# Encoder block on one core: first score map's buffers over other memory, distance copies later in a tile, meta columns by a two-input operation, four output rows in flight

## The chip, the cores and the metric

The kernel runs on one core of one Trainium2 chip. The metric is device time in microseconds (us) of one execution; lower is better. The engines are called as the profile calls them: PE (TensorE, matmuls and transposes), DVE (VectorE), ACT (ScalarE), POOL (GpSimd), and SP (SyncE), whose queue issues most DMAs.

## What is computed

One encoder block on 1024 tokens of width 1024, float32, with 16 meta tokens put in front. Two attention branches share one input: branch A is differential attention over all 1040 keys (4 heads, two score maps each), branch B is windowed attention with sinks (8 heads). Each branch is gated, both are added, and a SwiGLU network follows.

```python
h = concatenate([meta, x])                         # 1040 x 1024
p = rms_norm(h, norm_mix) @ w_in                   # qa ka va | qb kb vb | gate a, gate b
# branch A, head by head (two maps, m = 0 and m = 1)
s_m = q_m @ k_m.T * scale - slope * dist           # dist = |i - j|, 0 for meta keys
attn = softmax(s_0) - lam * softmax(s_1)
y_a = rms_norm(attn @ v, subln_g) * (1 - lambda_init)
# branch B: keys within 128 tokens and the meta keys, sink in the softmax
y_b = windowed_gqa(qb, kb, vb, sink)
h = h + (sigmoid(ga) * (y_a @ w_ba) + sigmoid(gb) * (y_b @ w_bb)) @ w_o
f = rms_norm(h, norm_ffn)
h = h + (silu(f @ w_ff_gate) * (f @ w_ff_up)) @ w_ff_down
out = rms_norm(h, norm_final)[16:]                 # 1024 rows of 1024
```

## The kernel before

Every float32 product is made of three matmuls of a high and a low part (fp32r); ACT makes the high part, DVE or POOL the low one. The large products follow Strassen's scheme with seven products instead of eight. The stages, by the time of the profile: projections and branch B up to about 275 us; branch A's attention together with the gate projections, 266 to 609 us; the branch products and the output projection to about 778 us; gate and up products of the feed-forward network to 1207 us; the down product, with the final norm and the output, to the end.

**Branch A** goes over 4 heads times 8 tiles of 128 queries. `scores_a(h, t)` makes the two maps of a tile, m = 1 first: PE writes three chunks of scores (352, 352 and 336 keys, L1049), two of them into the one pair of PSUM banks `two`, the third into one of three banks `sc`. DVE adds the distance bias and takes the minimum (L1052 for the two chunks, L1056 for the third), ACT takes the exponential (L1060). After m = 0, DVE combines both maps into the buffer of m = 0 (L1066) and copies the last 16 columns, the meta keys, twice behind it (L1070). A tile later `transpose_a` turns the result on PE (L1081); ACT and DVE split it (L1084, L1085), and PE multiplies it with the values (L1094).

The buffers of m = 1 come in turn from the pool `apool`. Those of m = 0 are two fixed tiles, `s0s` (`as0_0`, `as0_1`). `apool` lies where the pool of branch B (`bpool`) lay before it; where a new tile covers an old one, its first writer waits for the last user of the old tile. The order of allocation in `apool` thus decides what a tile waits for. In the kernel before, `s0s` comes behind the room of the transposed maps (`at`).

L1056 needs the distances of the last 336 keys in a form of their own, `far_m`, three tiles in turn. POOL fills them from `dist` (`far_copy`, L999), for a tile two tiles ahead; a copy waits until DVE has read the tile's content before.

**The gate projections** run in between: PE's order is written out by hand (`SLOTS`, one letter for a step: s scores, g a quarter of a gate product, t transposes, n values), with 63 gate products of 12 matmuls (L937). POOL makes their operands `wopg` (`weights_g`: sums at L816 and L817, a cast at L835, a low part at L836), from weights that SP loads (L795). The list `made_g` holds the low parts in order. Outside the orders written by hand a scheduler places the instructions, by a simulated timeline; `tc.issue_after(x)` puts what follows behind x.

**The end**: the down product's last step (p = 4) is finished row tile by row tile in `finish_last`: a sum of squares on ACT (L1843), the factor on POOL (L1870, L1871), then the two halves of an output row `o` on DVE (L1874) and ACT (L1876), each stored by its own DMA. Four earlier row tiles are finished in `evict`. Both take `o` from two buffers.

Of the kernel before, what the change touches and what calls it, by code (L numbers as in the profile page):

```python
# [9 lines left out]
F32 = mybir.dt.float32  # L10
# [4 lines left out]
ALU = mybir.AluOpType  # L15
# [4 lines left out]
P = 128  # L20
S = 1024
D = 1024
NM = 16
L = S + NM
DC = D // P
L_ROW = 1088
NT = S // P
# [13 lines left out]
SLOTS = "ssgsggntssgsggntgnt", "ssggsggntssgsggntgnt", "ssgsgnssgtsgntgnt"  # L41
N_PRE = 6
ON_ACT = (1, 6), (1, 7)
LAST_B = ("T1", 4), (5, "V0"), (5, "T2"), ("T2", 6), (7, "V1"), (7, "V2")
SLOTS_LAST = "ggggntgntnt"
S_BUFS = (2, 2)
# [31 lines left out]
def encoder_block(ctx: ExitStack, tc: tile.TileContext, x, meta, norm_mix, w_in, lq1, lk1, lq2, lk2,  # L78
                  subln, sink, w_ba, w_bb, w_o, norm_ffn, w_g, w_u, w_d, norm_final, out, dbg=None):
    nc = tc.nc  # L80
# [675 lines left out]
    apool, close_apool = pool("apool")  # L756
# [41 lines left out]
    sums_g, keys_a, raws_g, values_in, turned_t, made_g = {}, [], [], [], {}, []  # L798
# [190 lines left out]

    far_m = [(gstage if i > 1 else apool).tile([P, 336], F32, name=f"far_m{i}") for i in range(3)]  # L990
    apool.tile([P, 32], F32, name="apool_pad")
    apool.tile([P, 9, 2, 256], F32R, tag="at", name="at_room", bufs=AT_BUFS)

    def far_copy(n):
        if n < AH * NT:
            with ExitStack() as after:
                if n == 3:
                    after.enter_context(tc.issue_after(made_g[min(5, len(made_g) - 1)].ins))
                nc.gpsimd.tensor_copy(far_m[n % 3][:, 0:S - 704], dist[:, 1600 - n % NT * P:1600 - n % NT * P + S - 704])  # L999

    for i in range(3):
        nc.gpsimd.memset(far_m[i][:, S - 704:], 0.0)
        if i < 2:
            far_copy(i)
    s0s = [apool.tile([P, 9 * P], F32, name=f"as0_{i}") for i in range(2)]
    def load_a(h):
        p = kvpool
        qs, ks = [None, None], [None, None]
# [22 lines left out]
    def scores_a(h, t, ld, s):  # L1031
        slope = 2.0 ** -(2 * (h + 1))
        qs, ks, _ = ld
        nm = f"{h}_{t}"
        mn = small.tile([P, 2, 4], F32, tag="amn", name=f"amn_{nm}")
        dn = small.tile([P, 2], F32, tag="adn", name=f"adn_{nm}")
        if t % 4 == 0:
            sum_a[h, t // 4] = small.tile([P, 4], F32, tag="asum", name=f"asum_{nm}")
        first_sum = sum_a[h, t // 4][:, t % 4:t % 4 + 1]
        u0 = 896 - t * P  # L1040
        far = far_m[(h * NT + t) % 3]
        far_copy(h * NT + t + 2)
        for m in (1, 0):
            s[m] = s0s[t % 2] if m == 0 else apool.tile([P, L], F32, tag="s1", name=f"as1_{nm}", bufs=S_BUFS[1])
            two = psum2.tile([P, 2, 512], F32, tag="two", name=f"aps2_{nm}_{m}", bufs=1)
            for i, (k0, n) in enumerate(A_CHUNKS):
                ps = two[:, i] if i < 2 else bank(psum2, "sc", f"aps_{nm}_{m}", SC)
                for vv in range(2):
                    nc.tensor.matmul(ps[:, :n], qs[m][:, t * P:(t + 1) * P], ks[m][:, vv, k0:k0 + n],  # L1049
                                     start=(vv == 0), stop=(vv == 1))  # L1050
                if i == 1:
                    nc.vector.tensor_tensor_reduce(s[m][:, 0:2 * n].rearrange("p (a k) -> p a k", a=2), two[:, :, :n],  # L1052
                                                   dist[:, u0:u0 + 2 * n].rearrange("p (a k) -> p a k", a=2), slope, far_a,
                                                   ALU.add, ALU.min, mn[:, m, 0:1])
                elif i == 2:
                    nc.vector.tensor_tensor_reduce(s[m][:, k0:k0 + n], ps[:, :n], far, slope, mn[:, m, 0:1],  # L1056
                                                   ALU.add, ALU.min, mn[:, m, 1:2])
                if i < 2:
                    yield
            nc.scalar.activation(s[m][:, 0:L], s[m][:, 0:L], AF.Exp, bias=mn[:, m, 1:2], scale=-1.0,  # L1060
                                 accum_out=dn[:, 1:2] if m else first_sum)
            if m:
                nc.vector.reciprocal(dn[:, 1:2], dn[:, 1:2])
            yield
        nc.vector.tensor_scalar(dn[:, 0:1], first_sum, dn[:, 1:2], neglam, ALU.mult, ALU.mult)
        nc.vector.scalar_tensor_tensor(s[0][:, 0:L], s[1][:, 0:L], dn[:, 0:1], s[0][:, 0:L], ALU.mult, ALU.add)  # L1066
        with ExitStack() as after:
            if (h, t) == (0, 0):
                after.enter_context(tc.issue_after(made_g[min(5, len(made_g) - 1)].ins))
            nc.vector.tensor_copy(s[0][:, L:L + 2 * NM].rearrange("p (a k) -> p a k", a=2),  # L1070
                                  s[0][:, S:L].unsqueeze(1).broadcast_to([P, 2, NM]))

    def transpose_a(h, t, s, at_):
        i = t % 2
# [85 lines left out]
    for n in range(AH * NT + T_LAG):  # L1160
# [3 lines left out]
        if n < AH * NT:  # L1164
            h, t = divmod(n, NT)
# [289 lines left out]
    nf = len(order_f)  # L1455
# [375 lines left out]
    def evict(p, u):  # L1831

        half, col = TARGET[p]
        t, cols = 4 * half + u, slice(col * 512, col * 512 + 512)
        if p != 4 or not u:
            nc.vector.tensor_tensor(y[:, t, cols], y[:, t, cols], sets[BANKS[p]][u], ALU.add)
        yield
        if p in (2, 3, 7, 4):
            if t not in sums:
                sums[t] = upool.tile([P, 2], F32, name=f"ss_o{t}")  # L1840
            sq = upool.tile([P, 512], F32, tag="sq", name=f"sq_{t}_{col}", bufs=2)
            src = sets[BANKS[p]][u] if p == 4 and u else y[:, t, cols]
            nc.scalar.activation(sq, src, AF.Square, accum_out=sums[t][:, col:col + 1])  # L1843
            if p == 4:
                yield from finish_last(t, src)
                return
            yield
        if p == 7:

            nc.vector.tensor_tensor(y[:, t, cols], y[:, t, cols], nfin[:, cols], ALU.mult)  # L1850
            nc.vector.tensor_scalar(sums[t][:, 1:2], sums[t][:, 1:2], D * EPS, None, ALU.add)
        if p != 3:
            return
        ss = sums[t]
        o = upool.tile([P, D], F32, tag="o", name=f"o_{t}", bufs=2)
        r = small.tile([P, 1], F32, tag="rstd", name=f"rstd_o{t}")
        nc.vector.tensor_tensor(r, ss[:, 0:1], ss[:, 1:2], ALU.add)
        nc.vector.tensor_scalar(r, r, 1.0 / D, EPS, ALU.mult, ALU.add)
        nc.gpsimd.tensor_tensor(r, r, neg_half[:, 0:1], ALU.pow)
        yield  # L1860
        for i in range(2):
            at = slice(i * 512, i * 512 + 512)
            nc.vector.scalar_tensor_tensor(o[:, at], y[:, t, at], r, nfin[:, at], ALU.mult, ALU.mult)
        yield
        nc.sync.dma_start(out[t * P:(t + 1) * P, :], o)

    def finish_last(t, src):
# [2 lines left out]
        nc.gpsimd.tensor_scalar(r, ss[:, 0:1], ss[:, 1:2], 1.0 / D, ALU.add, ALU.mult)  # L1870
        nc.gpsimd.tensor_tensor(r, r, neg_half[:, 0:1], ALU.pow)  # L1871
        yield
        o = upool.tile([P, D], F32, tag="o", name=f"o_{t}", bufs=2)
        nc.vector.scalar_tensor_tensor(o[:, 0:512], src, r, nfin[:, 0:512], ALU.mult, ALU.mult)  # L1874
        nc.sync.dma_start(out[t * P:(t + 1) * P, 0:512], o[:, 0:512])
        nc.scalar.activation(o[:, 512:], y[:, t, 512:], AF.Copy, scale=r)  # L1876
# [7 lines left out]
    pending, running = [], []  # L1884
    for n in range(nf, len(steps)):
        p, j = steps[n][1]
        if n < nf + 4:

            prepare()
        while late:  # L1890
# [69 lines left out]
```

## Time and profile before

| | |
|---|---|
| median of 3 runs | 1417.67 us (1417.59 to 1417.71) |
| the profiled execution | 1418.93 us, of which the span from first to last instruction 1415.9 us |
| clock granted to PE | 0.999 |
| PE busy | 1398.6 us (99% of the span) |
| DVE, ACT, POOL busy | 939.8, 674.0, 667.0 us |
| DMA | 227.73 MB, mean 161 GB/s |

A row of the waits reads: engine, what waited, what it waited for: us in total, times, longest. A row of a timeline reads: start, duration, engine, line, operation, output<-input, shape, count, and in brackets how long the engine was idle ahead of it and for whom. A group's row ends with busy us, mean ns of one, and idle time ahead of it.

### The profile page before, as it was taken

How to read it: one execution, taken by the hardware profiler on the slowest of the kernel's cores; microseconds unless marked ns; L12 is line 12 of the kernel's file. 1: busy time of each engine (PE TensorE's matmuls, PEld its weight loads, DVE VectorE, ACT ScalarE, POOL GpSimd, SP SyncE). 2: the span in 40 equal slices, each digit the busy share in tenths (PEclk: the TensorE clock that was granted, in tenths of full speed). 3: DMA queues.
4: the chain of work that ended last, by engine and by line, in shares of the span. 5: the costliest groups of instructions: out<-in, count | busy, mean ns of one | idle time of the engine just before them, and what ended most of it. 6: DMA issues, size and time to landing. Idle time of an engine off the chain costs nothing.

```text
span 1415.9 us, 20684 instructions
## 1 busy us (share of the span) xinstructions
PE 1398.6 (99%) x7171; PEld 1199.3 (85%) x7171; DVE 939.8 (66%) x1619; ACT 674.0 (48%) x1285; POOL 667.0 (47%) x634
## 2 busy tenths in 40 slices
PE   9999999989999999999999999999999999999998
PEld 8989999878888888888888888888888888888886
DVE  6546666666677878666978956544455443787566
ACT  6346565545444545554446644333333333444454
POOL 4156884556777776522404055545555451000442
PEclk9999999999999999999999999999999999999999
DMA  8446658554896363395512634433233323954343
GB/s 240 92 118 194 185 176 295 160 164 127 284 305 207 115 209 100 120 334 170 183 63 108 190 106 142 140 112 103 97 106 106 103 102 101 369 178 142 120 127 141
DMA packets 193016, 227.73 MB, mean 161 GB/s; under 512 B 16952, under 2 KB 126464, under 8 KB 192784
## 3 DMA queue, kind: packets, MB, share of 16 engines
q1 hardware_dynamic: 190160, 222.80, 49.3%
q10 hardware_dynamic: 2752, 3.61, 0.8%
q8 instruction: 56, 0.92, 0.3%
q14 instruction: 48, 0.39, 0.1%
HBM read 152.48 MB, written 68.39 MB: 156 GB/s over the span
## 4 chain that ended last, share of the span: by engine, by line
PE 90%; DVE 4%; ACT 2%; issue 1%; DMA 1%; POOL 1%; SPq 0%; DVEq 0%; ACTq 0%; POOLq 0%
PE pg L1723 29%; PE pd L1827 14%; PE pg L937 8%; PE ppa L749 6%; PE po L1626 4%; PE pp_va L235 3%; PE pp_ka L235 3%; PE pp_qb L235 3%; PE aps L1049 3%; PE apy L1094 3%; PE bps L415 2%; PE pp_qa L235 2%; PE po L1634 2%; PE apt L1081 2%; PE bpy L462 1%
## 5 line engine op out<-in xcount | busy, mean ns | idle before, releaser
L1723 PE MATMUL pg<-t,wop 128*128 128x512 f32 x1056 | 242.5, 390 | 0.0
L1723 PEld LDWEIGHTS pg<-t,wop 128*128 128x128 f32 x1056 | 198.4, 188 | 41.0
L124 POOL TENSOR_TENSOR wop<-wf,wop 128x512 fp32r<-128x512 f32 x114 | 154.1, 1353 | 162.3 <-ACT wop L123 150.5
L1827 PE MATMUL pd<-ob,oa 128*128 128x512 f32 x924 | 209.9, 390 | 0.7 <-DVE ob L124 0.7
L1827 PEld LDWEIGHTS pd<-ob,oa 128*128 128x128 f32 x924 | 173.5, 188 | 37.0 <-DVE ob L124 1.1
L937 PE MATMUL pg<-hT_hi,wopg 128*128 128x512 f32 x488 | 183.1, 401 | 0.7 <-POOL wopg L836 0.6
L1723 PE MATMUL pg<-b,wop 128*128 128x512 f32 x792 | 183.3, 390 | 0.0
L1723 PEld LDWEIGHTS pg<-b,wop 128*128 128x128 f32 x792 | 148.5, 188 | 30.6
L1060 ACT ACTIVATE as<-as,amn 128x1040 f32<-128x1040 f32 x64 | 74.6, 1165 | 105.2 <-DVE amn L1056 99.7
L123 ACT ACTIVATE wop<-wf 128x512 fp32r<-128x512 f32 x128 | 80.8, 632 | 74.0 <-PE pg L1723 44.7
L124 POOL TENSOR_TENSOR oa<-ra,oa 128x512 fp32r<-128x512 f32 x27 | 34.9, 1294 | 169.7 <-ACT oa L123 168.2
L937 PEld LDWEIGHTS pg<-hT_hi,wopg 128*128 128x128 f32 x488 | 91.7, 188 | 15.4 <-POOL wopg L836 1.1
L123 ACT ACTIVATE oa<-ra 128x512 fp32r<-128x512 f32 x77 | 48.7, 632 | 108.5 <-PE pd L1827 49.0
L937 PE MATMUL pg<-hT_lo,wopg 128*128 128x512 f32 x244 | 96.0, 393 | 0.0
L1049 PE MATMUL aps<-ak,aq 128*128 128x352 f32 (+1 forms) x384 | 87.4, 336 | 4.5 <-DVE amn L1052 3.9
L1500 DVE TENSOR_TENSOR s<-wf,wf 128x512 f32<-128x512 f32 x22 | 16.3, 742 | 113.2 <-DMA wf<-in_w_ff_up_dram 69.9
L1049 PEld LDWEIGHTS aps<-ak,aq 128*128 128x128 f32 x384 | 63.0, 189 | 15.1 <-DVE amn L1052 9.0
L1052 DVE CUSTOM_DVE_ANT_0 as<-aps,dist,far_a 128x704 f32<-128x704 f32 x64 | 60.3, 942 | 21.8 <-PE aps L1049 15.9
L417 DVE CUSTOM_DVE_ANT_0 bs<-bps,tbx,nsink 128x432 f32<-128x432 f32 (+1 forms) x64 | 38.3, 627 | 45.2 <-PE bps L415 32.4
L427 POOL TENSOR_SCALAR bs<-bs,bdn 128x432 f32<-128x432 f32 (+1 forms) x64 | 37.0, 596 | 52.2 <-DVE bdn L425 31.7
L1094 PEld LDWEIGHTS apy<-at,av 128*128 128x128 f32 x400 | 54.1, 189 | 4.1
L1084 ACT ACTIVATE at<-apt 128x512 fp32r<-128x512 f32 (+1 forms) x96 | 46.2, 486 | 23.2 <-PE apt L1081 22.1
(340 smaller groups left out, 3141.5 us busy)
## 6 DMA issues: line engine op xcount, KB each, us to landing
ra<-aop SPq DMA_DIRECT2D x77, 256.0 KB, 2.7
wf<-in_w_ff_gate_dram SPq DMA_DIRECT2D x25, 512.0 KB, 3.9
wf<-in_w_ff_up_dram SPq DMA_DIRECT2D x25, 512.0 KB, 3.8
aop<-as SPq DMA_DIRECT2D x44, 256.0 KB, 2.1
wg_s<-in_w_in_dram SPq DMA_DIRECT2D x18, 512.0 KB, 4.3
aop<-c SPq DMA_DIRECT2D x33, 256.0 KB, 2.0
ak<-ka_d SPq DMA_DIRECT2D x16, 520.0 KB, 6.9
t_d<-tst SPq DMA_DIRECT2D x16, 512.0 KB, 4.8
```

Source lines behind the costliest of these rows:

```text
L123: high = nc.scalar.activation(hi, src, AF.Copy)
L124: lo_eng.tensor_tensor(lo, src, f32(hi), ALU.subtract)
L235: product = nc.tensor.matmul(ps[:, :n], a[:, c, :], b[:, c, at:at + n], start=(u == 0), stop=(u == 3 * DC - 1))
L749: nc.tensor.matmul(ps, w[:, a, j, :], src(j, b, tk), start=(j == 0 and n == 0), stop=(j == 3 and n == 2))
L937: product = nc.tensor.matmul(ps, op[:, x, c, :], h[:, 4 * d + c, HALF[t]], start=(p in (1, 6, 7) and c == 0 and i == 0), stop=(p in (2, 6, ...
L1049: nc.tensor.matmul(ps[:, :n], qs[m][:, t * P:(t + 1) * P], ks[m][:, vv, k0:k0 + n], start=(vv == 0), stop=(vv == 1))
L1052: nc.vector.tensor_tensor_reduce(s[m][:, 0:2 * n].rearrange("p (a k) -> p a k", a=2), two[:, :, :n], dist[:, u0:u0 + 2 * n].rearrange("p ( ...
L1060: nc.scalar.activation(s[m][:, 0:L], s[m][:, 0:L], AF.Exp, bias=mn[:, m, 1:2], scale=-1.0, accum_out=dn[:, 1:2] if m else first_sum)
L1094: nc.tensor.matmul(py[:, cols], v[:kp, a, k, :], at_[:kp, k, b, :], start=(k == 0 and j == 0), stop=(k == 8))
L1626: nc.tensor.matmul(sets_o[p][u], oa[:, a, u * P:(u + 1) * P], ob[:, b, :], start=(p in (1, 5) and j == 0 and k == 0), stop=(p in (2, 3) an ...
L1723: nc.tensor.matmul(ps, op[:, x, c, :], b[:, y, c, :], start=(p in (1, 5) and c == 0 and n == 0), stop=(p in (4, 2, 3) and c == 3 and n == ...
L1827: nc.tensor.matmul(ps[u], oa[:, a, u * P:(u + 1) * P], ob[:, b, :], start=(p in (1, 2, 5) and j == 0 and k == 0), stop=(p in (2, 3, 4) and ...
```

## The change

Four things, of which the second takes in two places.

1. `s0s` is allocated ahead of the room of the transposed maps, so it covers other memory of branch B, and the room of `at` moves up by as much.
2. The copy of distances is called in the m = 0 half of a tile instead of ahead of the m = 1 half. The copies for tiles 3, 4 and 5 are put behind the newest gate operand; before, only the one for tile 3 was put behind the sixth operand.
3. The meta columns are written by a `scalar_tensor_tensor` that takes the same columns as both inputs, max(1.0 * x, x), instead of a copy. The rule that put the first of them behind a POOL operation goes.
4. The output rows have four buffers instead of two, and in the down product's first steps `prepare()` is called early for 8 steps instead of 4.

```diff
+FAR_LATE = 6
...
     apool.tile([P, 32], F32, name="apool_pad")
+    s0s = [apool.tile([P, 9 * P], F32, name=f"as0_{i}") for i in range(2)]
     apool.tile([P, 9, 2, 256], F32R, tag="at", name="at_room", bufs=AT_BUFS)
...
-                if n == 3:
-                    after.enter_context(tc.issue_after(made_g[min(5, len(made_g) - 1)].ins))
+                if 2 < n < FAR_LATE:
+                    after.enter_context(tc.issue_after(made_g[-1].ins))
                 nc.gpsimd.tensor_copy(far_m[n % 3][:, 0:S - 704], dist[:, 1600 - n % NT * P:1600 - n % NT * P + S - 704])
...
-    s0s = [apool.tile([P, 9 * P], F32, name=f"as0_{i}") for i in range(2)]
...
-        far_copy(h * NT + t + 2)
         for m in (1, 0):
+            if m == 0:
+                far_copy(h * NT + t + 2)
...
-        with ExitStack() as after:
-            if (h, t) == (0, 0):
-                after.enter_context(tc.issue_after(made_g[min(5, len(made_g) - 1)].ins))
-            nc.vector.tensor_copy(s[0][:, L:L + 2 * NM].rearrange("p (a k) -> p a k", a=2),
-                                  s[0][:, S:L].unsqueeze(1).broadcast_to([P, 2, NM]))
+        more, last = s[0][:, L:L + 2 * NM].rearrange("p (a k) -> p a k", a=2), s[0][:, S:L].unsqueeze(1).broadcast_to([P, 2, NM])
+        nc.vector.scalar_tensor_tensor(more, last, 1.0, last, ALU.mult, ALU.max)
...
-        o = upool.tile([P, D], F32, tag="o", name=f"o_{t}", bufs=2)
+        o = upool.tile([P, D], F32, tag="o", name=f"o_{t}", bufs=4)
...
-        if n < nf + 4:
+        if n < nf + 8:
```

(The line with `o` changes in both `evict` and `finish_last`.) The orders of PE and ACT are the same in both kernels; on DVE, POOL and SP some instructions move.

DVE at the first tile of branch A, from the m = 0 scores on, with the semaphores that each row waits for; `as0_0` is the buffer of m = 0, `as1_0_1` the m = 1 buffer of tile 1. Before:

```order
L1052 ISA as0_0_3441,amn_0_0_3534<-aps2_0_0_0_3560,dist_852,far_a_873 128x704 [waits DMAHW7_49,PE_49]
L1052 ISA amn_0_0_3534 128x1
L1056 ISA as0_0_3441,amn_0_0_3534<-aps_0_0_0_3572,far_m0_3431,amn_0_0_3534 128x336 [waits DVE_49,PE_49]
L1056 ISA amn_0_0_3534 128x1
L1063 RECIPROCAL adn_0_0_3535<-adn_0_0_3535 128x1 [waits Activation_49]
L1065 TENSOR_SCALAR adn_0_0_3535<-asum_0_0_3536,adn_0_0_3535,neglam_882 128x1 [waits DVE_49,Activation_49]
L1066 SCALAR_TENSOR_TENSOR as0_0_3441<-as1_0_0_3538,adn_0_0_3535,as0_0_3441 128x1040 [waits DVE_49]
L1070 COPY as0_0_3441<-as0_0_3441 128x32 [waits DVE_49]
L1052 ISA as1_0_1_3605,amn_0_1_3602<-aps2_0_1_1_3606,dist_852,far_a_873 128x704 [waits PE_49]
```

The same place in the changed kernel, where the lines of this function have moved by two:

```order
L1054 ISA as0_0_3435,amn_0_0_3534<-aps2_0_0_0_3560,dist_852,far_a_873 128x704 [waits PE_49]
L1054 ISA amn_0_0_3534 128x1
L1058 ISA as0_0_3435,amn_0_0_3534<-aps_0_0_0_3572,far_m0_3431,amn_0_0_3534 128x336 [waits DVE_49,PE_49]
L1058 ISA amn_0_0_3534 128x1
L1065 RECIPROCAL adn_0_0_3535<-adn_0_0_3535 128x1 [waits Activation_49]
L1067 TENSOR_SCALAR adn_0_0_3535<-asum_0_0_3536,adn_0_0_3535,neglam_882 128x1 [waits DVE_49,Activation_49]
L1068 SCALAR_TENSOR_TENSOR as0_0_3435<-as1_0_0_3537,adn_0_0_3535,as0_0_3435 128x1040 [waits DVE_49]
L1070 SCALAR_TENSOR_TENSOR as0_0_3435<-as0_0_3435 128x32 [waits DVE_49]
L1054 ISA as1_0_1_3604,amn_0_1_3602<-aps2_0_1_1_3605,dist_852,far_a_873 128x704 [waits PE_49]
```

The wait for a DMA is gone from the first row, and the copy has become a two-input operation.

POOL at the same time; `wopg_3_6` is the operand of gate product (3, 6), `wg_f3_0` and `wg_f3_1` are its loaded weights, `far_m0`, `far_m1`, `far_m2` the distances for tiles 3, 4 and 5. Before:

```order
L1180 MEMSET as0_0_3441 128x80 [waits DMAHW7_49,DMAHW4_49,DVE_49]
L1180 MEMSET as0_1_3442 128x80 [waits PE_49,Activation_49]
L835 CAST wopg_2_2_3595<-wg_f2_0_3466 128x512 [waits PE_49]
L999 COPY far_m0_3431<-dist_852 128x320 [waits DVE_49]
L836 TENSOR_TENSOR wopg_2_2_3595<-wg_f2_0_3466,wopg_2_2_3595 128x512 [waits Pool_49]
L835 CAST wopg_3_1_3633<-wg_f3_0_3479 128x512 [waits DMAHW6_49,PE_49]
L999 COPY far_m1_3432<-dist_852 128x320 [waits DVE_49]
L836 TENSOR_TENSOR wopg_3_1_3633<-wg_f3_0_3479,wopg_3_1_3633 128x512 [waits Pool_49]
L816 TENSOR_TENSOR wg_f3_1_3520<-wg_f3_1_3520 128x512 [waits DMAHW1_49]
L817 TENSOR_TENSOR wg_f3_1_3520<-wg_f3_1_3520,wg_f3_0_3479 128x512 [waits Pool_49]
L835 CAST wopg_3_6_3678<-wg_f3_1_3520 128x512 [waits PE_49,Pool_49]
L999 COPY far_m2_3433<-dist_852 128x320 [waits DVE_49]
```

In the changed kernel:

```order
L1179 MEMSET as0_0_3435 128x80
L1179 MEMSET as0_1_3436 128x80
L836 CAST wopg_2_2_3595<-wg_f2_0_3466 128x512 [waits PE_49]
L837 TENSOR_TENSOR wopg_2_2_3595<-wg_f2_0_3466,wopg_2_2_3595 128x512 [waits Pool_49]
L836 CAST wopg_3_1_3632<-wg_f3_0_3479 128x512 [waits DMAHW6_49,PE_49]
L837 TENSOR_TENSOR wopg_3_1_3632<-wg_f3_0_3479,wopg_3_1_3632 128x512 [waits Pool_49]
L1001 COPY far_m0_3431<-dist_852 128x320 [waits DVE_49]
L817 TENSOR_TENSOR wg_f3_1_3520<-wg_f3_1_3520 128x512 [waits DMAHW1_49]
L818 TENSOR_TENSOR wg_f3_1_3520<-wg_f3_1_3520,wg_f3_0_3479 128x512 [waits Pool_49]
L836 CAST wopg_3_6_3678<-wg_f3_1_3520 128x512 [waits PE_49,Pool_49]
L837 TENSOR_TENSOR wopg_3_6_3678<-wg_f3_1_3520,wopg_3_6_3678 128x512 [waits Pool_49]
L1001 COPY far_m1_3432<-dist_852 128x320 [waits DVE_49]
```

The memsets have lost all their waits, and each of the three copies stands one to four operand steps later. From the seventh copy on POOL's order is the same.

On SP, the load of `wg_f_0` for gate pair (8, .) stands behind two loads of `ak_0` and one of a saved partial sum, which followed it before. On DVE, beside the exchanged operation, six small rows of the first tiles change places with a neighbour. At the end nothing moves; the third and fourth output row of `finish_last` lose a wait for a DMA on DVE and on ACT.

More of the change, by code (lines that the diff above doesn't have):

```diff
@@ L1872, in finish_last @@
         yield
-        o = upool.tile([P, D], F32, tag="o", name=f"o_{t}", bufs=2)
+        o = upool.tile([P, D], F32, tag="o", name=f"o_{t}", bufs=4)
         nc.vector.scalar_tensor_tensor(o[:, 0:512], src, r, nfin[:, 0:512], ALU.mult, ALU.mult)
```

## The prediction

> **What bounds the kernel now.** I read the page first (share of each engine, chain that ended last), then the busy time by stretch, then the waits and the timelines of the stretches in which TensorE is not full.
>
> ```profile
> span 1415.9 us, 20684 instructions
> PE 1398.6 (99%) x7171; PEld 1199.3 (85%) x7171; DVE 939.8 (66%) x1619; ACT 674.0 (48%) x1285; POOL 667.0 (47%) x634
> PE 90%; DVE 4%; ACT 2%; issue 1%; DMA 1%; POOL 1%; SPq 0%; DVEq 0%; ACTq 0%; POOLq 0%
> ```
>
> TensorE (PE) bounds it: 1398.6 of 1415.9 us. The change touches no matmul, so it can win only from the 17.3 us in which PE is idle, and it can lose only by adding to them. Where they lie, by stretch (columns: stretch, length, PE, PEld, DVE, ACT, POOL, clock, DMA share, GB/s):
>
> ```profile
> 280.00:290.00 10.00, 8.39 (x41) 6.93 (x40) 2.70 (x9) 3.57 (x6) 6.96 (x10) 1.00 0.97 314
> 290.00:300.00 10.00, 9.43 (x49) 7.45 (x47) 7.65 (x15) 4.13 (x8) 3.46 (x5) 1.00 0.69 214
> 300.00:310.00 10.00, 8.26 (x44) 6.81 (x43) 8.57 (x20) 4.83 (x9) 7.00 (x6) 1.00 0.21 66
> 310.00:320.00 10.00, 10.00 (x65) 9.18 (x65) 7.09 (x18) 4.57 (x8) 8.05 (x9) 1.00 0.37 120
> ```
>
> 3.9 us are lost between 280 and 310 us, where the first maps of branch A are scored; from 310 on PE is full. The waits there (PEld is the weight load of a matmul), and the timeline of DVE:
>
> ```profile
> DVE as L1052 <- DMA yb_d<-by: 5.7, 1, 5.7
> PEld aps L1049 <- DVE amn L1052: 3.3, 3, 2.0
> ```
>
> ```profile
> 286.40 0.95 DVE L1052 CUSTOM_DVE_ANT_0 as<-aps,dist,far_a 128x704 f32<-128x704 f32 x1 [5.70 <-DMA yb_d<-by]
> 289.76 1.74 DVE L1066 SCALAR_TENSOR_TENSOR as<-as,adn,as 128x1040 f32<-128x1040 f32 x1
> ```
>
> DVE stands still for 5.70 us, since the buffer `as0_0`, the m = 0 half of the first score map, covers a staging tile of branch B whose store (`yb_d<-by`) has not landed. PE has gate products to run meanwhile, then waits behind DVE several times.
>
> **The head: buffers over other memory.** The order of the changed kernel shows that the DMA is gone from the wait of this instruction; the wait for PE that is left is for its own scores. What it is worth I read from PE's starts:
>
> ```profile
> 285.19 0.39 PE L937 MATMUL pg<-hT_lo,wopg 128*128 128x512 f32 x1
> 285.42 0.39 PE L937 MATMUL pg<-hT_hi,wopg 128*128 128x512 f32 x1
> 287.41 0.91 PE L1049 MATMUL aps<-ak,aq 128*128 128x352 f32 x4 [1.61 <-DVE amn L1052]
> 292.64 0.92 PE L1049 MATMUL aps<-ak,aq 128*128 128x352 f32 x4 [0.42 <-DVE amn L1052]
> 296.95 0.89 PE L1049 MATMUL aps<-ak,aq 128*128 128x352 f32 x4
> 301.58 0.66 PE L1081 MATMUL apt<-ident,as 128*128 128x128 f32 x4 [1.34 <-DVE at L1085]
> 302.64 0.92 PE L1049 MATMUL aps<-ak,aq 128*128 128x352 f32 x4 [0.40 <-DVE amn L1052]
> 318.34 0.89 PE L1049 MATMUL aps<-ak,aq 128*128 128x352 f32 x4
> 321.81 0.89 PE L1049 MATMUL aps<-ak,aq 128*128 128x352 f32 x4
> ```
>
> The idle times in brackets sum to 1.61 + 0.42 + 1.34 + 0.40 = 3.77 us. They count from modelled ends; start to start there is more. Gate matmuls follow each other by 285.42 - 285.19 = 0.23, so the scores at 287.41 could have come at 285.65: 1.76 lost. Tile 4 goes from its m = 1 scores to its m = 0 scores in 321.81 - 318.34 = 3.47 with nine gate matmuls between them; tile 2 has the same list and takes 302.64 - 296.95 = 5.69: 2.22 lost. Tile 1 has twelve gate matmuls there, so 3.47 + 3 x 0.23 = 4.16 against 292.64 - 287.41 = 5.23: 1.07 lost. Together 5.05 us.
>
> How much of it goes? Without the stall, DVE takes the m = 0 scores of tile 0 at about 281.4, five microseconds earlier. Each later PE wait is for DVE, and PE itself reaches these places only 1.76, 2.83 and 5.05 us earlier, so DVE gains more than PE takes up at the first two. At the third, the transposes of tile 1 (301.58 now, 297.2 then), the combination L1066 of tile 1 and the low part L1085 behind it have to be through. DVE would reach that L1066 at about 294.5; L1066 takes 1289 to 2430 ns (rows below), L1085 about 0.6, so they end at 296.4 to 297.5, and the next map's L1052 0.9 later. That leaves 0 to 0.9 us of wait; I take 0.4. Head: 5.05 - 0.4 = **4.6 us**, bounds 3.5 (the bracketed sum, less about a third of a microsecond) and 5.05.
>
> **What would be late next.** The gate products need operands from POOL. Now the copy of distances for tile 3 stands on POOL ahead of one operand's second half, the copy for tile 4 ahead of another's, and both wait for DVE.
>
> ```profile
> 286.40 0.27 POOL L1180 MEMSET as<- 128x80 f32 x2 [1.90 <-DMA yb_d<-by]
> 296.87 0.45 POOL L999 COPY far_m<-dist 128x320 f32<-128x320 f32 x1 [6.46 <-DVE amn L1056]
> 306.01 1.30 POOL L836 TENSOR_TENSOR wopg<-wg_f,wopg 128x512 fp32r<-128x512 f32 x1
> 307.66 0.40 PE L937 MATMUL pg<-hT_hi,wopg 128*128 128x512 f32 x1
> 287.23 0.41 SPq L795 DMA_DIRECT2D wg_f<-in_w_in_dram x1
> wg_f<-in_w_in_dram SPq DMA_DIRECT2D x6, 512.0 KB, 6.2
> ```
>
> The operand (3, 6) is ready at 306.01 + 1.30 = 307.31, and PE takes it at about 307.7 to 308.1: under 1 us of room. Five microseconds earlier on PE (302.6 or later) it would be short, had the copies stayed where they are. In the new order they stand behind these halves, and the memsets wait for nothing. Then the operand hangs on its weights: issued on SP at 287.23 behind stores that still wait for the same branch B store, so not earlier than now; with the median 6.2 us of this window landed at 293.4; two sums of 1.3, a cast of 0.6 and a difference of 1.3 follow: 298 to 300 with some port waits. Room of 2.6 to 4.6 us. So the later copies are worth nothing by themselves, but without them part of the head would be taken back. The copies themselves come at about 291 and 300, and DVE reads them at about 305 and 315.
>
> Further on, SP now issues one weight load behind two key loads and a saved partial sum:
>
> ```profile
> 352.58 0.40 SPq L795 DMA_DIRECT2D wg_f<-in_w_in_dram x1
> ak<-ka_d SPq DMA_DIRECT2D x16, 520.0 KB, 6.9
> 361.18 1.28 POOL L836 TENSOR_TENSOR wopg<-wg_f,wopg 128x512 fp32r<-128x512 f32 x1
> 366.38 0.39 PE L937 MATMUL pg<-hT_hi,wopg 128*128 128x512 f32 x1
> ```
>
> Two times 520 KB and 256 KB are 1.33 MB; at 314 GB/s (the stretch from 280 us) that is 4.2 us. The operand made from this load is ready at 361.18 + 1.28 = 362.46, and PE takes it at 366.38. With all of the 4.2 us it would come at 366.7, 0.3 too late; since the load flows beside the others, I take 0 and keep 0.3 as its bound.
>
> **Meta columns by a two-input operation.** The rows (min/median/max ns) of the copy that goes, of the combination in front of it, and of the same kind of operation as the new one, one SBUF tile as both inputs:
>
> ```profile
> L1070 DVE COPY as<-as x32: 164/299/1261, 291.5 to 586.2; 128x32 f32<-128x32 f32 x32
> L1066 DVE SCALAR_TENSOR_TENSOR as<-as,adn,as x32: 1289/1302/2430, 289.8 to 584.1; 128x1040 f32<-128x1040 f32 x32
> L1111 DVE SCALAR_TENSOR_TENSOR ae<-asum x8: 151/229/909, 316.7 to 583.5; 128x4 f32<-128x4 f32 x8
> L1070 DVE COPY as<-as 128x32 f32<-128x32 f32 x32 | 15.4, 480 | 0.0
> L1111 DVE SCALAR_TENSOR_TENSOR ae<-asum 128x4 f32<-128x4 f32 x8 | 2.4, 302 | 0.0
> PEld aps L1049 <- DVE amn L1052: 5.7, 9, 1.1
> ```
>
> All three are stretched at times, by up to 0.8 to 1.1 us. Base of the new one: 151 ns and 28 elements more at (1289 - 151)/1036 = 1.1 ns, 0.18 us; with L1111's mean stretch (302 - 151) 0.33, with the copy's own (480 - 164) 0.50. Per operation that is -0.15 to +0.02 us against 0.48. PE feels DVE at the nine waits of the last row (from 425 us on) and two on transposes: 11 x -0.15 = -1.6 to 11 x 0.02 = +0.2 us. The Trainium skill (SBUF — State Buffer, section "Who interferes with whom") says that a DVE instruction with two SBUF inputs contends with a GpSimd instruction that reads SBUF, as one in a two-port mode does with any. By that rule the new form escapes only GpSimd's writes, and the term is 0; were it wrong, the sum would be 1.6 us lower. L1066, with two SBUF inputs and stretched to 2430, agrees. I take **0**, since L1066 is the nearest two-input row in the same place.
>
> **The tail: four output rows.**
>
> ```profile
> 1410.02 0.75 DVE L1874 SCALAR_TENSOR_TENSOR o<-pd,rstd_o,nfin 128x512 f32<-128x512 f32 x1 [2.04 <-DMA out_dram<-o]
> 1411.31 0.75 DVE L1874 SCALAR_TENSOR_TENSOR o<-pd,rstd_o,nfin 128x512 f32<-128x512 f32 x1 [0.54 <-DMA out_dram<-o]
> 1410.15 0.55 POOL L1871 TENSOR_TENSOR rstd_o<-rstd_o,neg_half 128x1 f32<-128x1 f32 x1
> 1411.30 0.72 ACT L1876 ACTIVATE o<-y,rstd_o 128x512 f32<-128x512 f32 x1 [0.57 <-DMA out_dram<-o]
> ```
>
> The last row waits for the store two rows before it. With four buffers it waits for POOL's factor instead, ready at 1410.70: DVE starts 0.57 earlier, ACT, which first does the row before and issues its store, about 0.5. Tail: **0.5 us**, bounds 0.4 and 0.57. The wider `n < nf + 8` moves no instruction on any engine: 0.
>
> **Sum.** 4.6 + 0 + 0.5 = 5.1 us. The profiled execution took 1418.93 (span 1415.9 and 3.0 around it) and would take 1413.8; the median of the runs, 1417.67, lies 1.26 below it, so 1412.6. Bounds of the terms: -(5.05 + 0.57 + 1.6) = 1410.5 and -(3.5 + 0.4 - 0.2 - 0.3) = 1414.3.
>
> **Rivals.**
> *The chain of DVE catches PE again.* Only the first wait goes (1.76), DVE's own work (8.57 of 10 us from 300 on) keeps the others. With the tail 1417.67 - 2.26 = 1415.4. For it: that busy share; against it: DVE gets 5.7 us, more than PE takes. 0.14.
> *The buffers land on another late tile.* The wait moves, only the tail is left: 1417.2. Against it: no DMA stands in the new wait. 0.03.
> *The two-input form escapes the port.* 1.6 less: 1411.0. Against it L1066's own 2430. 0.07.
> *Slower: the two-input form is stretched as L1111's longest, 909 ns, in every tile.* 32 x (0.909 - 0.480) = 13.7 us on DVE; if all of it reached PE, 1412.6 + 13.7 = 1426.3. It outweighs the gains from a mean of 0.48 + 5.1/32 = 0.64 us on. For it: DVE is nearly full in some windows late in the stage; against it: L1111's median 229. 0.08.
>
> **How the numbers follow.** The forecast has 0.68. About 0.2% (2.8 us) can be told from no change here, so faster means under 1414.8. The forecast and the escape lie there (0.75), with a little of the first rival (0.02): faster 0.77; the rest of that rival and the moved wait: same 0.15; slower 0.08. Likeliest alone: 1410.5 to 1414.3; the range reaches on to the first rival, 1415.4.
>
> **What would show it.** Right: no DVE wait on `yb_d` near 281; PE's brackets there gone or below 0.9 us; tile 2's m = 1 scores at about 294; the operand (3, 6) ready before PE wants it; the last L1874 behind POOL instead of a DMA; L1070 again with a mean of 0.3 to 0.5 us. Wrong: PE waiting for POOL between 298 and 305, the DVE waits of tiles 1 and 2 still there, or PE waits after 425 us longer than now.

## The result, and the profile after

The changed kernel takes 1411.30 us (median of 6 runs, 1410.71 to 1412.95); the kernel before took 1417.97 us in 6 runs of the same measurement (1417.59 to 1420.03). The ratio is 0.9953, 95% interval 0.9940 to 0.9966: faster by 0.47%. Forecast were 1412.6 us and a range of 1410.5 to 1415.4. The profiled execution took 1410.71 us, 1408.9 of them its span. The page after:

```profile
PE 1397.5 (99%) x7171; PEld 1199.4 (85%) x7171; DVE 939.9 (67%) x1619; ACT 673.9 (48%) x1285; POOL 665.6 (47%) x634
PE 92%; DVE 4%; ACT 2%; issue 1%; POOL 1%; DMA 0%; SPq 0%; ACTq 0%; DVEq 0%; POOLq 0%
```

PE idles for 11.4 us instead of 17.3, and DMA has gone from the chain that ended last (1% before). The same stretches as in the prediction (length, PE, PEld, DVE, ACT, POOL, clock, DMA share, GB/s):

```profile
280.00:290.00 10.00, 10.00 (x51) 8.53 (x51) 6.50 (x14) 4.74 (x7) 8.27 (x10) 1.00 0.94 301
290.00:300.00 10.00, 10.00 (x55) 8.67 (x54) 8.71 (x20) 5.33 (x12) 8.59 (x10) 1.00 0.82 253
300.00:310.00 10.00, 10.00 (x58) 8.76 (x57) 7.28 (x19) 4.28 (x9) 4.49 (x5) 1.00 0.42 125
```

PE is full in all three; before it had 8.39, 9.43 and 8.26. The first rows of branch A in the timelines of DVE and PE, in order of time:

```profile
281.35 0.95 DVE L1054 CUSTOM_DVE_ANT_0 as<-aps,dist,far_a 128x704 f32<-128x704 f32 x1 [0.75 <-PE aps L1051]
284.67 1.42 DVE L1068 SCALAR_TENSOR_TENSOR as<-as,adn,as 128x1040 f32<-128x1040 f32 x1
285.60 0.80 PE L1051 MATMUL aps<-ak,aq 128*128 128x352 f32 x4
294.28 1.53 DVE L1068 SCALAR_TENSOR_TENSOR as<-as,adn,as 128x1040 f32<-128x1040 f32 x1
295.74 0.68 DVE L1084 TENSOR_TENSOR at<-apt,at 128x512 fp32r<-128x512 f32 x1
297.08 0.60 PE L1080 MATMUL apt<-ident,as 128*128 128x128 f32 x4
297.44 0.89 PE L1051 MATMUL aps<-ak,aq 128*128 128x352 f32 x4
```

DVE takes the m = 0 scores at 281.35 instead of 286.40, after 0.75 us for PE instead of 5.70 for a store. PE's rows that had waited (287.41, 301.58 and 302.64 before) start at 285.60, 297.08 and 297.44 and have no brackets. The end:

```profile
1403.75 0.55 POOL L1870 TENSOR_TENSOR rstd_o<-rstd_o,neg_half 128x1 f32<-128x1 f32 x1
1404.34 0.75 DVE L1873 SCALAR_TENSOR_TENSOR o<-pd,rstd_o,nfin 128x512 f32<-128x512 f32 x1 [1.28 <-POOL rstd_o L1870]
1404.39 0.72 ACT L1875 ACTIVATE o<-y,rstd_o 128x512 f32<-128x512 f32 x1 [0.47 <-POOL rstd_o L1870]
```

Both halves of the last row now wait for POOL's factor and not for a store.

Where the 7.0 us of the span went is read at four rows of PE's timeline: the first and the last 128x352 scores of branch A, the first output projection matmul, and PE's last group, whose start and duration give its end. First before, then after:

```profile
277.58 0.81 PE L1049 MATMUL aps<-ak,aq 128*128 128x352 f32 x4
578.42 0.91 PE L1049 MATMUL aps<-ak,aq 128*128 128x352 f32 x4
696.07 2.20 PE L1626 MATMUL po<-ob_o,oa_o 128*128 128x512 f32 x9
1389.78 19.20 PE L1827 MATMUL pd<-ob,oa 128*128 128x512 f32 x84
```

```profile
277.48 0.80 PE L1051 MATMUL aps<-ak,aq 128*128 128x352 f32 x4
573.09 0.92 PE L1051 MATMUL aps<-ak,aq 128*128 128x352 f32 x4
690.68 7.64 PE L1625 MATMUL po<-ob_o,oa_o 128*128 128x512 f32 x33
1389.73 12.85 PE L1826 MATMUL pd<-ob,oa 128*128 128x512 f32 x56
```

| stretch, us | before | after | difference |
|---|---|---|---|
| start to the first scores of branch A | 277.58 | 277.48 | -0.10 |
| first to last scores of branch A | 300.84 | 295.61 | -5.23 |
| to the first output projection matmul | 117.65 | 117.59 | -0.06 |
| from there to PE's end | 712.91 | 711.90 | -1.01 |
| tail behind PE's end | 6.92 | 6.32 | -0.60 |

The 1.01 us is no term of the prediction. It is one stall at the start of the down product, where DVE waits for weights (before, then after):

```profile
1201.00 3.46 SPq L1519 DMA_DIRECT2D wd_c<-in_w_ff_down_dram  x5
1205.28 0.69 DVE L1546 TENSOR_TENSOR wd_a<-wd_c,ra 128x512 f32<-128x512 f32 x1 [4.72 <-DMA wd_c<-in_w_ff_down_dram]
1209.57 0.69 DVE L124 TENSOR_TENSOR ob<-ra,ob 128x512 fp32r<-128x512 f32 x1
1210.31 3.06 PE L1827 MATMUL pd<-ob,oa 128*128 128x512 f32 x12 [0.69 <-DVE ob L124]
```

```profile
1195.63 2.60 SPq L1518 DMA_DIRECT2D wd_c<-in_w_ff_down_dram  x5
1199.02 0.69 DVE L1545 TENSOR_TENSOR wd_a<-wd_c,ra 128x512 f32<-128x512 f32 x1 [3.83 <-DMA wd_c<-in_w_ff_down_dram]
1202.80 0.68 DVE L125 TENSOR_TENSOR ob<-ra,ob 128x512 fp32r<-128x512 f32 x1
```

Before, the first of these loads was issued at 1201.00 and DVE had its data at 1205.28, 4.28 us later; after, 3.39 us later. For the third of the loads DVE waited 0.81 us, where it is 0.19 after. The operand `ob` that PE wanted at 1210.31 was ready at 1209.57 + 0.69 = 1210.26, 9.26 us behind the first load's issue; after it was ready 7.85 us behind it, and PE took it without a wait.

### The profile page after: what moved, and what is told of

Its sections match the earlier page's. It is cut to its first block, busy times and chain, and to the rows that moved or that the text cites. A ratio compares the mean times of both kernels' runs of the same rounds, so it can differ in the third digit from the quotient of the medians.

```text
span 1408.9 us, 20675 instructions
## 1 busy us (share of the span) xinstructions
PE 1397.5 (99%) x7171; PEld 1199.4 (85%) x7171; DVE 939.9 (67%) x1619; ACT 673.9 (48%) x1285; POOL 665.6 (47%) x634
## 4 chain that ended last, share of the span: by engine, by line
PE 92%; DVE 4%; ACT 2%; issue 1%; POOL 1%; DMA 0%; SPq 0%; ACTq 0%; DVEq 0%; POOLq 0%
PE pg L1722 30%; PE pd L1826 15%; PE pg L938 9%; PE ppa L750 6%; PE po L1625 4%; PE aps L1051 3%; PE pp_va L236 3%; PE pp_ka L236 3%; PE pp_qb L236 3%; PE apy L1093 2%; PE bps L416 2%; PE pp_qa L236 2%; PE po L1633 2%; PE apt L1080 2%; PE bpy L463 1%; PE bpt L457 1%
## 5 line engine op out<-in xcount | busy, mean ns | idle before, releaser
L125 POOL TENSOR_TENSOR wop<-wf,wop 128x512 fp32r<-128x512 f32 x114 | 151.2, 1326 | 164.8 <-ACT wop L124 152.8
L1749 ACT COPY p<-pg 128x512 f32<-128x512 f32 x44 | 25.8, 587 | 66.5 <-PE pg L1722 66.5
```

What stands on the lines that cost most here:

```text
L125: lo_eng.tensor_tensor(lo, src, f32(hi), ALU.subtract)
```

## The experiments

One execution of a kernel differs from the next by up to 5 us (the kernel before took 1418.9 to 1419.9 us in the median beside these runs); up to 2.7 us of it lie ahead of branch A, whose first scores came at 277.5 to 280.2 us in the profiles. Each kernel has one profile, the kernel before and the changed one have two. Terms below 1 us are therefore read from the stretches of the table above. Times are medians; each ratio is to the kernel before on the same chip in the same measurement.

| kernel | time (runs) | ratio, 95% | branch A | to PE's end | tail |
|---|---|---|---|---|---|
| e1: the move alone | 1413.26 (5) | 0.9958 (0.9945 to 0.9970) | 295.57 | 712.19 | 6.97 |
| e2: copies early | 1411.16 (5) | 0.9946 (0.9932 to 0.9959) | 295.70 | 712.28 | 6.30 |
| e3: meta copied | 1411.72 (5) | 0.9951 (0.9938 to 0.9963) | 295.69 | 712.19 | 6.28 |
| e4: two rows | 1413.46 (5) | 0.9961 (0.9948 to 0.9973) | 296.18 | 712.24 | 7.05 |
| b1: before again | 1420.14 (1) | | 301.09 | 712.69 | 7.02 |
| e5: no move | 1417.45 (11) | 0.9987 (0.9978 to 0.9995) | 300.14 | 711.89 | 6.34 |
| e6: meta twice | 1413.16 (5) | 0.9956 (0.9944 to 0.9968) | 297.06 | 712.55 | 6.36 |
| e7: meta on ACT | 1408.62 (5) | 0.9922 (0.9908 to 0.9936) | 292.89 | 711.90 | 6.31 |
| a1: after again | 1411.79 (5) | 0.9946 (0.9933 to 0.9958) | 295.59 | 712.22 | 6.36 |
| e8: e7 and a step on DVE | 1410.29 (5) | 0.9932 (0.9919 to 0.9944) | 293.03 | 712.53 | 6.56 |
| e11: all copies late | 1410.65 (5) | 0.9936 (0.9922 to 0.9949) | 293.49 | 711.94 | 6.32 |
| e9: e7 and e11 | 1407.10 (5) | 0.9918 (0.9904 to 0.9932) | 291.89 | 711.90 | 6.39 |

**The move alone (e1).** The kernel before with one line moved:

```diff
     apool.tile([P, 32], F32, name="apool_pad")
+    s0s = [apool.tile([P, 9 * P], F32, name=f"as0_{i}") for i in range(2)]
     apool.tile([P, 9, 2, 256], F32R, tag="at", name="at_room", bufs=AT_BUFS)
```

> The kernel before with only the m = 0 buffers moved ahead of the room of the transposed maps; the distance copies stand on POOL where they stood before. The prediction's step says that without the later copies part of the head is taken back: PE reaches the operand (3, 6) about 5 us earlier, and with the operand late PE waits 0.5 to 2 us for POOL between 298 and 305 us, so 1413 to 1414.5. The rival: the copy in front of this operand waits for DVE, and DVE comes 5 us earlier as well, so the operand comes at about 302.2 where PE wants it at 302.4; nothing is taken back, PE is 5.2 us earlier from 303 us on, and the time is 1411.3 to 1412.6 (the tail keeps its two-row wait, 0.6 us, against the changed kernel).

The whole head is there: branch A takes 295.57 us, as in the changed kernel, and only the tail is still 6.97. On POOL the operand (3, 6) again stands behind a distance copy that waits for DVE:

```profile
301.64 0.45 POOL L1000 COPY far_m<-dist 128x320 f32<-128x320 f32 x1 [2.10 <-DVE amn L1056]
302.06 1.29 POOL L836 TENSOR_TENSOR wopg<-wg_f,wopg 128x512 fp32r<-128x512 f32 x1
303.67 0.62 PE L937 MATMUL pg<-hT_hi,wopg 128*128 128x512 f32 x2
```

The copy starts 3.95 us earlier than before (301.64 against 305.59), since the DVE row that it waits for moved too; the operand is ready at 302.06 + 1.29 = 303.35 instead of 307.31. PE's third matmul of this product, the first that needs the low part, starts at 303.67 and has no bracket. The rival holds: nothing is taken back, though only 0.3 us of room is left. The median alone, 1413.26, would fit the other range (1413 to 1414.5); but the five runs reach from 1411.54 to 1414.91, so the stretch decides and not the median.

**The copies back in their old place (e2).**

```diff
-                if 2 < n < FAR_LATE:
-                    after.enter_context(tc.issue_after(made_g[-1].ins))
+                if n == 3:
+                    after.enter_context(tc.issue_after(made_g[min(5, len(made_g) - 1)].ins))
...
+        far_copy(h * NT + t + 2)
         for m in (1, 0):
-            if m == 0:
-                far_copy(h * NT + t + 2)
```

> The changed kernel with the distance copies back where they stood before. By the prediction's step 0.5 to 2 us of the head are taken back by PE waits for POOL between 298 and 305 us: 1411.8 to 1413.3. By the rival (the copies move with DVE) PE loses at most 0.3 us there: 1411.3 to 1411.6.

295.70 us for branch A against 295.61 and 295.59 in two profiles of the changed kernel: the later copies of tiles 3 to 5 are worth nothing here.

**The meta columns copied again (e3).**

```diff
-        nc.vector.scalar_tensor_tensor(more, last, 1.0, last, ALU.mult, ALU.max)
+        nc.vector.tensor_copy(more, last)
```

> The changed kernel with the meta columns copied again by a one-input copy, in the same place. If the two-input form is worth nothing (the prediction's term 0): mean of the copy 0.45 to 0.55 us, time 1411.3 within 0.4. If the two-input form escapes the port: PE waits after 425 us get longer, up to 1412.9. If the one-input copy is the shorter one: down to 1410.9.

The groups by line, of this kernel and of the changed one (busy us, mean ns):

```profile
L1070 DVE COPY as<-as 128x32 f32<-128x32 f32 x32 | 16.1, 504 | 0.0
```

```profile
L1070 DVE SCALAR_TENSOR_TENSOR as<-as 128x32 f32<-128x32 f32 x32 | 16.5, 515 | 0.0
```

504 and 515 ns, and 295.69 against 295.61 us: both forms are stretched alike, and neither is better.

**Two output rows (e4).**

```diff
-        o = upool.tile([P, D], F32, tag="o", name=f"o_{t}", bufs=4)
+        o = upool.tile([P, D], F32, tag="o", name=f"o_{t}", bufs=2)
```

(In both places.)

> The changed kernel with two output row buffers instead of four. If the tail's term is right, the last DVE row waits for a store again and the time is 0.4 to 0.6 us longer: 1411.7 to 1411.9, all of it behind PE's last matmul. If the row buffers were worth nothing: 1411.3. PE's stall of 1.0 us at 1210 us in the profile of before (late weights) should have nothing to do with it: it is there or not by chance.

The tail is 7.05 us again, and the last row waits for a store (DVE):

```profile
1406.22 0.75 DVE L1873 SCALAR_TENSOR_TENSOR o<-pd,rstd_o,nfin 128x512 f32<-128x512 f32 x1 [0.46 <-DMA out_dram<-o]
```

Its branch A took 296.18 us, 0.5 longer than the same code in the changed kernel, with one bracket of 0.21 us for DVE at 298.38. In this execution DVE's combination of tile 1 (L1068) took 2.22 us instead of 1.53, beside two additions of POOL (L817, L818) that came 2.4 us later than in the changed kernel. That is how far one execution can stray in this stage. The median rose by more than the tail (1413.46, where 1411.7 to 1411.9 was expected). The profiled run took 2.0 us more than that of the changed kernel: 0.7 of them in the tail, 0.6 in branch A, 0.4 ahead of it and 0.3 between the output projection and PE's end.

**The kernel before, profiled again (b1).**

> The kernel before, profiled a second time. If the stall of PE at 1210 us (late weights of the down product) belongs to this kernel, it is there again and the stretch from the first output projection matmul to PE's last is 712.9 us; if it is chance, that stretch is 711.9 to 712.3 us as in the changed kernels. The stretch from the first to the last scores of branch A should be 300.8 us again, the tail behind PE's last matmul 6.9.

Branch A 301.09, the tail 7.02, and the stall at 1210 is there again, with 0.47 us. It was also seen, with 0.35 and 0.22 us, in e6 and e8, which have the moved buffers, and not in e5, which has them in the old place. So it does not hang on the place of the buffers alone. It was longest in the two profiles of before; what decides whether these weights come late stays open.

**All but the move (e5).** The allocation of `s0s` back behind `at_room`; the three other parts stay:

```diff
-    s0s = [apool.tile([P, 9 * P], F32, name=f"as0_{i}") for i in range(2)]
     apool.tile([P, 9, 2, 256], F32R, tag="at", name="at_room", bufs=AT_BUFS)
...
+    s0s = [apool.tile([P, 9 * P], F32, name=f"as0_{i}") for i in range(2)]
     def load_a(h):
```

> The changed kernel with the m = 0 buffers back behind the room of the transposed maps; late distance copies, two-input meta columns and four output rows stay. By the prediction the head is lost whole: DVE waits 5 to 6 us for the store of branch B, the stretch from the first to the last scores is 300.8 us instead of 295.6, and only the tail's 0.6 us is left against before: 1417.1 (and 1 us less if the stall at 1210 is chance and stays away). Rival, the late copies carry part of the head by themselves: 299 to 300 us for that stretch.

The wait is back, on DVE:

```profile
288.24 0.95 DVE L1054 CUSTOM_DVE_ANT_0 as<-aps,dist,far_a 128x704 f32<-128x704 f32 x1 [5.79 <-DMA yb_d<-by]
```

Branch A takes 300.14 us, so the move carries 4.5 of the 5.2 us. Against 300.84 and 301.09 in the two profiles of before, 0.7 to 0.95 us are gained without the move, as the rival had it in part. DVE's combination of tile 1 shows where, first before, then in e5:

```profile
298.50 2.43 DVE L1066 SCALAR_TENSOR_TENSOR as<-as,adn,as 128x1040 f32<-128x1040 f32 x1
298.53 1.30 POOL L816 TENSOR_TENSOR wg_f<-wg_f 128x512 f32<-128x512 f32 x1
```

```profile
300.72 1.30 DVE L1068 SCALAR_TENSOR_TENSOR as<-as,adn,as 128x1040 f32<-128x1040 f32 x1
302.68 0.66 PE L1080 MATMUL apt<-ident,as 128*128 128x128 f32 x4 [0.25 <-DVE at L1084]
```

Before, POOL stood 6.46 us in the copy for tile 4 (the row at 296.87 in the prediction), and the second operation behind that copy, an addition (L816), then fell on the combination, which took 2.43 us (2.42 in b1). With the copies later, the same addition (L817 in e5) runs at 295.08, ahead of the combination, which takes 1.30 us, and PE's wait at the transposes of tile 1 is 0.25 us instead of 1.34. So the late copies hold this gain as far as these rows tell; e5 has the other two parts as well, and no run has the late copies alone. With e1 and e2, where the copies are worth nothing once the move is made, the two gains don't add.

**What DVE's time is worth (e6, e7).** The step on the meta columns issued twice, and the same step taken off DVE:

```diff
         nc.vector.scalar_tensor_tensor(more, last, 1.0, last, ALU.mult, ALU.max)
+        nc.vector.scalar_tensor_tensor(more, last, 1.0, last, ALU.mult, ALU.max)
```

```diff
-        nc.vector.scalar_tensor_tensor(more, last, 1.0, last, ALU.mult, ALU.max)
+        nc.scalar.activation(more, last, AF.Copy)
```

> The changed kernel with the operation on the meta columns issued twice (the second writes the same values). It adds 32 x 0.2 to 0.5 us to DVE. By the prediction's pricing each of eleven waits of PE for DVE takes the whole of it: 11 x 0.5 = 5.7 us longer for a stretched second one, 2 us for an unstretched one. Rival: only the three waits that stop PE itself (0.20, 0.40, 0.96 us) take it: 0.6 to 1.5 us longer, so 1412 to 1412.8. In the second of a pair POOL's instruction should have ended, so its mean should be 0.2 to 0.3 us.

> The changed kernel with the meta columns copied by ACT instead of DVE. DVE loses 16.5 us. If the operation is on PE's path at the waits for DVE, they shorten: up to 1.6 us faster, 1409.7 to 1411. Rival: the copy stands on ACT behind DVE's combination and holds up the exponential behind it, so the waits stay or grow: 1411.3 to 1413. ACT's copy should not be stretched: 0.2 us each.

The second one of e6 (L1071), by line:

```profile
L1071 DVE SCALAR_TENSOR_TENSOR as<-as 128x32 f32<-128x32 f32 x32 | 19.0, 594 | 0.1
```

19.0 us more on DVE cost 1.45 us in branch A (297.06 - 295.61); eleven waits that take 594 ns each would be 6.5. For the stage the rival with three waits holds (0.6 to 1.5); the median, 1413.16, lies above its 1412 to 1412.8. The expected 0.2 to 0.3 us for the second of a pair was wrong: it was stretched more than the first (484). With the step on ACT, by line, and then the waits of PE from 425 us on, first after, then e7:

```profile
L1070 ACT ACTIVATE as<-as 128x32 f32<-128x32 f32 x32 | 7.4, 232 | 21.5 <-DVE as L1068 21.5
```

```profile
PEld aps L1051 <- DVE amn L1054: 5.5, 9, 1.2
PE aps L1051 <- DVE amn L1054: 1.2, 2, 1.0
PE apt L1080 <- DVE amn L1058: 0.4, 1, 0.4
```

```profile
PEld aps L1051 <- DVE amn L1054: 2.8, 5, 0.6
PE aps L1051 <- DVE amn L1054: 0.3, 1, 0.3
```

The step takes 232 ns on ACT and is not stretched. Branch A takes 292.89 us, 2.7 less than after (293.03 in e8, which has the same step on ACT); PE's own waits for DVE late in the stage are nearly gone, and the time is 1408.62 us, below the expected 1409.7 to 1411. In the changed kernel PE's own waits for DVE add up to only 1.6 us there, but they count from modelled ends. Matched start by start, six places between 459 and 566 us gain 3.1 us where the brackets read 1.8, the largest 1.21 us where the bracket reads 0.96. Smaller losses elsewhere take some of it back, the largest 0.3 us at a new wait of PE for DVE (the 0.3 in the last row, at 486.11). ACT's wait for L1068 (21.5 us) did not undo the gain. DVE's mean for L1068 was 1686 ns here, against 1545 after; in e9, with the same step on ACT, it was 1396, so the longer combination is no fixed price of taking the step off DVE.

**The changed kernel again (a1).**

> The changed kernel again, with a second profile. Stages as before: 295.6 us from the first to the last scores of branch A, 711.9 to 712.3 from the first output projection matmul to PE's last, tail 6.3. If the stall at 1210 us (0.35 to 0.7 us) hangs on this kernel's place in time it stays away again; if it is chance it may show. Median 1411.3 within 0.8.

All stretches as before, and no stall at 1210.

**One step of the factor on DVE (e8).** On top of e7:

```diff
-        nc.gpsimd.tensor_scalar(r, ss[:, 0:1], ss[:, 1:2], 1.0 / D, ALU.add, ALU.mult)
+        nc.vector.tensor_scalar(r, ss[:, 0:1], ss[:, 1:2], 1.0 / D, ALU.add, ALU.mult)
         nc.gpsimd.tensor_tensor(r, r, neg_half[:, 0:1], ALU.pow)
```

> The changed kernel with the meta columns on ACT and the first step of the last rows' factor on DVE instead of POOL (DVE stands idle there for 1.3 us ahead of the last row). The first step on POOL takes 0.27 us, on DVE 0.16 to 0.27; with the way from ACT to the engine the same, the tail gets 0.1 to 0.3 us shorter: 6.0 to 6.2 us. Stage of branch A 293 us as with the meta columns on ACT alone. Median 1408.3 within 0.8. Rival: the step waits on DVE behind something in its queue and the tail stays at 6.3.

```profile
1402.70 0.21 DVE L1869 TENSOR_SCALAR rstd_o<-ss_o 128x1 f32<-128x1 f32 x1 [1.17 <-ACT sq L1842]
1403.06 0.55 POOL L1870 TENSOR_TENSOR rstd_o<-rstd_o,neg_half 128x1 f32<-128x1 f32 x1 [1.49 <-DVE rstd_o L1869]
1403.75 0.72 ACT L1875 ACTIVATE o<-y,rstd_o 128x512 f32<-128x512 f32 x1 [0.47 <-POOL rstd_o L1870]
```

A miss: DVE is done at 1402.91, but POOL starts only at 1403.06, and from the start of DVE's step to the start of POOL's second it is 0.36 us, against 0.35 with both on POOL (1403.40 to 1403.75 after). The way between the engines eats the shorter step. The tail is 6.56 us, not 6.0 to 6.2, but its 0.24 us above the 6.32 of after are not the step's: ACT's last row starts 1403.75 - 1401.94 = 1.81 us behind PE's end, as it does after (1404.39 - 1402.58), and what is longer comes behind it, where the last store is issued and lands. The median, 1410.29, misses the expected 1408.3 within 0.8 too; this profile has 0.22 us of the stall at 1210.

**All distance copies late (e11), and both findings together (e9).** The rule behind the newest operand for every tile; e9 has the line of e7 as well:

```diff
-FAR_LATE = 6
+FAR_LATE = 32
```

> The changed kernel with the rule for the distance copies of tiles 3 to 5 (behind the newest gate operand) extended to all tiles. PE's one wait for POOL in the stage (0.64 us at 438 us) has behind it a POOL row that waits 3.5 us for DVE in a distance copy. If copies cost PE anything, this is where: with the copy elsewhere the wait goes and the time is 0.6 us lower, 1410.7. Rival: the copy stands in front of another operand and new waits for POOL come, 1411.3 to 1413.

> Both findings together: meta columns on ACT and all distance copies behind the newest gate operand. Of the waits of PE left with the meta columns on ACT (0.62 us for POOL at 440 us, 0.29 for DVE) the first goes: stage of branch A 292.3 us instead of 292.9, median 1408.0 within 0.8. Rival: with PE earlier the copies block another operand and a new wait for POOL takes its place: 293 us or more, 1408.6 or more.

POOL's waits in the copies and PE's for POOL from 425 us on, first after, then e11:

```profile
POOL far_m L1001 <- DVE amn L1058: 29.3, 13, 3.9
PE pg L938 <- POOL wopg L837: 0.6, 1, 0.6
```

```profile
POOL far_m L1001 <- DVE amn L1058: 12.7, 5, 4.0
PE aps L1051 <- DVE amn L1054: 0.7, 2, 0.4
PE apt L1080 <- DVE amn L1058: 0.3, 1, 0.3
```

The copies wait less than half as long, PE's wait for POOL has gone, and branch A takes 293.49 us, 2.1 less than after, where that wait alone made 0.6 expected; PE's waits for DVE went down as well, from 1.2 + 0.4 us (rows of after above) to 0.7 + 0.3, and so did the mean of the combination L1068, from 1545 to 1442 ns. The time is 1410.65 us, as expected. Once the buffers are moved, late copies are worth something here, and not at the three tiles that the change treats. With both, branch A takes 291.89 us (expected 292.3) and the time is 1407.10 us. Its ratio to before, 0.9904 to 0.9932, lies just below that of the changed kernel measured again, 0.9933 to 0.9958.

## Why the prediction was right, and where its steps were not

**The head** was right in cause and a little small: 4.6 us forecast, bounds 3.5 to 5.05. PE's scores at 302.64 come at 297.44, 5.20 earlier, of which 0.10 had been gained ahead of the stage: 5.1. The term kept 0.4 us for a wait at the transposes of tile 1 that did not remain. It forecast L1066 at 294.5 and the ends of L1085 at 296.4 to 297.5; they came at 294.28 and 295.74 + 0.68 = 296.42, the early end, and PE went through at 297.08. The 0.4 was not idle caution: in e4, where the same combination took 2.22 us instead of 1.53, PE's scores behind these transposes came 0.6 us later. The move alone gave all of it (e1), and without it 4.5 of it went (e5).

**The late copies** were a wrong step. The claim that part of the head would be taken back without them held the operand at 307.31 and moved only PE. But the copy in front of it waits for DVE, and so moves with DVE; e1 and e2 lost nothing. The forecast of the operand itself was a little late: 298 to 300, and it was ready at 296.36 + 1.29 = 297.65, 4.8 us before PE's first matmul of this product (302.43). POOL had its weights by 292.06 and not by 293.4.

```profile
296.36 1.29 POOL L837 TENSOR_TENSOR wopg<-wg_f,wopg 128x512 fp32r<-128x512 f32 x1
```

**The load behind the keys** cost nothing, as forecast, but it did come later: the operand made from it was ready 2.1 us before PE took it (359.05 and 361.15), where before there had been 3.9 (362.46 and 366.38). So 1.8 of the bound's 4.2 us were lost, and the room held them.

**The meta columns**: worth 0, as forecast; mean 515 ns against a forecast of 0.3 to 0.5 us. That both forms are held up, and by what, is seen, after, in the step's durations (min/median/max ns) and in a pair of rows of POOL and DVE:

```profile
L1070 DVE SCALAR_TENSOR_TENSOR as<-as x32: 169/310/1275, 286.1 to 580.8; 128x32 f32<-128x32 f32 x32
285.07 2.17 POOL L837 TENSOR_TENSOR wopg<-wg_f,wopg 128x512 fp32r<-128x512 f32 x1
286.12 1.16 DVE L1070 SCALAR_TENSOR_TENSOR as<-as 128x32 f32<-128x32 f32 x1
```

A step whose shortest took 169 ns lasts 1.16 us here, to within 0.05 us of the end of a POOL operation (287.24 and 287.28). Thirteen of the 32 steps last over 0.4 us, and each of the thirteen ends within 0.11 us of the end of a POOL operation; in e3, with the one-input copy, it is thirteen of thirteen as well. The Trainium skill (SBUF — State Buffer, section "Who interferes with whom") calls the pair of ports that DVE shares with GpSimd an exclusive lock, and counts a two-input operation and a one-input one in a two-port mode among those that take it; e3's 504 ns and these 515 ns agree. It gives ACT ports of its own, and e7's 232 ns agree.

What was wrong in this part is the price. The bounds of the term, and the rival in which the new form escapes the port, took it that PE feels every nanosecond at eleven waits. Freeing 515 ns gave 2.7 us instead of 11 x 0.515 = 5.7, and adding 594 ns cost 1.45 instead of 6.5. A price for one nanosecond on DVE does not follow from the two, since they differ.

**The tail**: 0.5 forecast, 0.60 measured (in the other runs 6.97 to 7.05 with two rows, 6.28 to 6.39 with four, e8 aside). DVE's last row starts 1404.34 - 1402.58 = 1.76 us behind PE's end, before it was 1411.31 - 1408.98 = 2.33: the 0.57 of the upper bound.

**What the sum lacked** is the stall of late weights at 1210 us, 1.0 us in the profile of before. It was on the list of PE's waits and belongs to no part of the change. Of the difference between forecast (1412.6) and result (1411.3), 0.5 is the head, 0.1 the tail, and the rest, 0.7, is of the size of that stall. As far as the profiles show, this last part is chance and no gain of the change. Of the rivals none came: no wait of PE for DVE remained at 287 to 303 us, and the two-input form was neither better nor worse.

## What to carry to other kernels

Where an allocation puts a first tile over one whose last user is a store, the order of allocation alone can be worth microseconds: look in the waits for an engine that waits for a store of a stage long past. When a wait is taken away, move everything that hangs on the engine that had waited, the copies on a third engine too, before claiming that one of them is late next. And a short operation that shares a port with a busy engine is priced by that engine's operations and not by its own size; putting it on an engine with free time (here ACT) did more than changing its form.

## What the runs showed of the hardware that was not expected

A DVE operation of 0.17 us can last 1.27 (169 and 1275 ns in the row above), and a POOL operation 2.17 instead of 1.29: in the pair shown above, POOL's operation lies under DVE's combination (284.67 + 1.42 = 286.09) and ends 1.15 us behind that one, and the meta step ends with it, as if the three had run one behind the other. In e6 the second of two such steps in a row was held up more than the first (594 against 484 ns); why was not settled. The large combination beside them has another mean in each of these kernels: 1545 ns after, 1686 with the step on ACT, 1442 with all copies late, 1396 with both. That what POOL runs beside it makes the difference was followed for one tile alone (2.43 us before, 1.30 in e5). Handing the first of two one-column steps from POOL to DVE gained nothing: 0.36 us from step to step against 0.35.
